# A seven-product feed-forward on one NeuronCore: six PSUM banks, norm matmuls placed later, and the last pass's operands made a pass ahead

## The chip, the core and the metric

The kernel runs on one core of a Trainium2 chip. The core's engines run side by side and meet through semaphores: TensorE (PE: matmuls, and PEld its weight loads), VectorE (DVE), ScalarE (ACT), GpSimd (POOL) and SyncE (SP), which here issues nearly all transfers between device memory and the on-chip buffers. Matmuls write into PSUM, eight banks of 128 x 512 fp32; all other operands lie in SBUF. The metric is the device time of one execution in microseconds. Three executions of the kernel before took 2996.5, 3001.04 and 3000.42 us; the median is 3000.42.

## What is computed

One layer of a decoder trunk on 2048 prompt tokens and 32 sample tokens, width 1024, all in fp32:

```python
sh1, sc1, g1, sh2, sc2, g2 = adaln_mods(c, lw['w_ada'], lw['b_ada'])
h = rms_norm(x, lw['norm1_g']) * (1 + sc1) + sh1
m, states = mixer(h)
x = x + g1 * m
h2 = rms_norm(x, lw['norm2_g']) * (1 + sc2) + sh2
x = x + g2 * swiglu(h2, lw['w_ffn_in'], lw['w_ffn_out'])
```

The mixer is one input projection, then sliding-window attention beside a gated causal convolution, a merge of the two and an output projection. swiglu(h) is (silu(g) * u) @ w_ffn_out, with g and u the halves of h @ w_ffn_in and 2816 hidden columns. A final RMSNorm closes it.

## The kernel before

**Numbers.** An fp32 matmul is made of three: each operand is split into a high half that the matmul takes exactly and the low rest, and hi x hi, hi x lo and lo x hi are summed in one PSUM bank (gemm, L483). The split of a weight is an ACT copy (L236, wh) and a POOL subtract (L237, wl).

**Stages.** Tokens come in two groups: g=0 has 1024 tokens, g=1 has 1024 and the 32 samples. For each group come the input projection, attention and convolution, and mixer_out (L1398), whose last product "wo" goes through three chunks of columns and leaves x2, the input of the feed-forward, in the tiles called third, or spilled to device memory as x2s. The feed-forward runs in three passes over the tokens: pass 0 holds chunks 0 and 1 of group 0 (2 x 336 columns), pass 1 chunk 2 of group 0 and chunk 0 of group 1, pass 2 chunks 1 and 2 of group 1 (2 x 352 columns each). Pass 0 runs ahead of group 1's mixer.

**Seven products.** A pass treats its two column blocks and the two halves of the 1024 input rows as a 2 x 2 block matrix, and the two halves of w_ffn_in likewise, and multiplies them with seven products in place of eight. For each hidden tile f, f_gate (L1735) makes products p1, p2, p6, p7, p5, p3, p4 in this order, each 4 x 3 = 12 matmuls into one bank, and VectorE adds them up into u, ga and ub on the way out of the bank. Weight combinations (the sums s and wr, w_part, L261) are made by VectorE from the raw weight when it has landed; the combinations of the activations, seven operands of four row tiles with a high and a low half each, are made once a pass by f_build (L1653) from the normed x2. f_down (L1781) takes pairs of hidden tiles through w_ffn_out: 16 banks of 6 matmuls, each added into x2 (residual, L1515). The blocks run as G1 (f_gate) of tiles 2p, then G2 (f_down) of pair p-1, then G1 of 2p+1 (ffn_order, L437).

**Norms.** The RMS of a chunk is a set of small matmuls of the squares sq with mean_d (rv_gen, L1564), a power on POOL, a diagonal matrix dg on VectorE, and a matmul with ones that spreads the factors over the partitions (f_rows, L1585). f_value (L1596) makes one normed, modulated tile of x2. h_second (L824) is the same for the input norm of group 1, in three chunks.

**PSUM.** Pool mm has four banks (all gemms, products and f_down tiles), ps two (norms, finals) and pt two (transposes: attention, x blocks, finals). A tile of a pool waits until the one that last had its bank has been read.

**What sets the order.** The order on each engine is written out by the program: the generators run in steps, one step wherever pump() (L452) is called, which is after every product or bank. Background generators (bg) step while a model of VectorE's time is not too far ahead of a model of PE's; tasks step once in task_dt ns of PE's modelled time. A "yield None" means that a generator waits for the next call. Instructions stand on an engine in the order in which they are issued, so a later yield puts an instruction behind more matmuls. All PE and VectorE operations go through one wrapper and have line 98 in the profile, so tiles' names tell them apart. After the last f_down of passes 0 and 1, the final norm of that pass's columns (final, L1858) runs as a task beside the next stage: transposes into a ps and a pt bank, squares on ACT, power on POOL, then scaling by ACT (L1894) and POOL (L1895, y) and stores on SP. At the last block but one of pass 1, build_next(2) (L1642) starts f_build(2), whose x2 fetches are issued by ACT (x2_fetch, L1615).

## Time and profile before

| | |
|---|---|
| median of three runs | 3000.42 us (2996.5 to 3001.04) |
| profiled execution, own time | 2991.93 us |
| its span, first to last instruction | 2989.8 us |
| mean granted PE clock | 0.971 of full |
| entry into pass 0 | about 700 to 780 us |
| steady pass 0 | 780 to 1200 us |
| first norm of group 1 begins | about 1200 us |
| entry into pass 1, steady | 1860 to 1950, 1950 to 2400 us |
| entry into pass 2, steady | 2400 to 2530, 2530 to 2900 us |

The page of the profile lists busy time of each engine, the span in 40 slices, the DMA queues, the chain of work that ended last and the costliest groups of instructions. Views of the trace add busy time in chosen stretches, what ended the waits of one engine in a stretch (engine, tile and line it waited for, us in total, times, longest), the chain in order of time, and the instructions in order of time. A wait is put down to the operation that came last. Shape: the slices of PE show the stage boundaries as dips between long stretches near full use:

```profile
PE   8988899999899999897889999799999977999998
PEclk9999999999999999998999999999999998999999
```

### The profile page before, as it was taken

The page shows a single profiled execution, that of the slowest core. Times are in us where ns is not written, and L with a number is a line of the kernel's source. Part 1 is how long each engine was busy: PE and PEld are TensorE (multiplying, and loading weights), DVE is VectorE, ACT ScalarE, POOL GpSimd, SP SyncE. Part 2 cuts the span into 40 slices and gives each one's busy share as a digit, 9 for nine tenths or more (in the row PEclk, how much of TensorE's full clock was granted, in tenths as well). Part 3 has the DMA queues.
Part 4 walks back from the last instruction along what each step waited for, and adds up shares of the span by engine and source line. Part 5 has one row for each costly group of instructions (what it writes and reads, how often), then busy time and mean ns, then how long its engine had stood idle before and what let it go on. Part 6 is the DMA issues. An engine that isn't in the chain of part 4 may idle for free. (4 is left out here: it accounts for less than half of the span.)

```text
span 2989.8 us, 43420 instructions
## 1 busy us (share of the span) xinstructions
PE 2743.9 (92%) x16046; PEld 2572.6 (86%) x16046; DVE 2054.2 (69%) x3320; ACT 1187.0 (40%) x2410; POOL 1649.5 (55%) x1289
## 2 busy tenths in 40 slices
PE   8988899999899999897889999799999977999998
PEld 4766677888799999897888999799999967999998
DVE  5999952466756666779997345766666676677676
ACT  4333465433433333432655343443333334333333
POOL 1366766333766567455674212476655647656654
PEclk9999999999999999998999999999999998999999
DMA  7542223443222222431112344332222224222222
GB/s 278 160 109 65 85 85 106 151 134 115 79 81 68 71 78 71 132 94 38 47 58 79 93 135 144 115 109 71 78 64 71 78 89 127 71 71 71 78 64 68
DMA packets 348472, 282.74 MB, mean 95 GB/s; under 512 B 31691, under 2 KB 304983, under 8 KB 348237
## 3 DMA queue, kind: packets, MB, share of 16 engines
q1 hardware_dynamic: 329189, 252.94, 27.6%
q10 hardware_dynamic: 19072, 27.03, 2.8%
q8 instruction: 127, 2.08, 0.3%
q14 instruction: 84, 0.69, 0.1%
HBM read 239.89 MB, written 40.14 MB: 94 GB/s over the span
## 5 line engine op out<-in xcount | busy, mean ns | idle before, releaser
L237 POOL TENSOR_TENSOR wl<-wr,wh 128x512 fp32r<-128x512 f32 (+1 forms) x470 | 890.1, 1908 | 684.6 <-ACT wh L236 624.5
L98 PE MATMUL mm<-third,wh 128*128 128x352 f32 (+1 forms) x3512 | 863.9, 326 | 60.8 <-DVE u L98 31.7
L98 PEld LDWEIGHTS mm<-third,wh 128*128 128x128 f32 x3512 | 615.9, 190 | 77.8 <-DVE u L98 40.0
L98 PE MATMUL mm<-third,wl 128*128 128x352 f32 (+1 forms) x1796 | 580.3, 323 | 0.0
L236 ACT ACTIVATE wh<-wr 128x512 fp32r<-128x512 f32 (+1 forms) x470 | 372.8, 811 | 373.0 <-PE mm L98 211.0
L98 PE MATMUL mm<-hh,wh 128*128 128x352 f32 (+1 forms) x1200 | 435.5, 363 | 28.8 <-DVE u L98 9.1
L98 PE MATMUL mm<-mh,wh 128*128 128x352 f32 (+1 forms) x1396 | 450.7, 323 | 4.3 <-DVE third L98 1.7
L98 PE MATMUL mm<-ml,wh 128*128 128x352 f32 (+1 forms) x1396 | 444.9, 322 | 0.0
L98 PE MATMUL mm<-hh,wl 128*128 128x352 f32 (+1 forms) x1200 | 425.5, 355 | 0.0
L237 POOL TENSOR_TENSOR wl<-s,wh 128x512 fp32r<-128x512 f32 x198 | 255.8, 1301 | 292.5 <-ACT wh L236 292.5
L98 PE MATMUL mm<-hl,wh 128*128 128x352 f32 (+1 forms) x1200 | 415.6, 355 | 0.6 <-DVE hl L98 0.6
L98 DVE SCALAR_TENSOR_TENSOR third<-mm,mod_G,third 128x352 f32<-128x352 f32 (+2 forms) x576 | 315.2, 568 | 143.8 <-PE mm L98 121.8
L98 DVE SCALAR_TENSOR_TENSOR dw<-u,cw,dw 128x1024 f32<-128x1024 f32 x240 | 395.2, 1660 | 4.7
L98 PE MATMUL mm<-mh,wl 128*128 128x336 f32 (+1 forms) x1044 | 334.9, 321 | 7.6 <-POOL wl L237 7.6
L98 PEld LDWEIGHTS mm<-third,wl 128*128 128x128 f32 x1796 | 341.2, 190 | 0.0
L98 DVE TENSOR_TENSOR u<-mm,u 128x352 f32<-128x352 f32 (+1 forms) x330 | 168.2, 515 | 165.8 <-PE mm L98 158.5
L98 PEld LDWEIGHTS mm<-hh,wh 128*128 128x128 f32 x1200 | 229.7, 191 | 60.7 <-issue 11.3
L236 ACT ACTIVATE wh<-s 128x512 fp32r<-128x512 f32 x198 | 120.7, 626 | 394.9 <-PE mm L98 251.5
L98 PEld LDWEIGHTS mm<-mh,wh 128*128 128x128 f32 x1396 | 265.5, 190 | 6.5 <-DVE third L98 2.0
L98 PEld LDWEIGHTS mm<-ml,wh 128*128 128x128 f32 x1396 | 264.1, 190 | 0.0
L98 PEld LDWEIGHTS mm<-hh,wl 128*128 128x128 f32 x1200 | 228.9, 191 | 21.6
L98 PEld LDWEIGHTS mm<-hl,wh 128*128 128x128 f32 x1200 | 228.2, 192 | 22.4 <-DVE hl L98 1.2
(333 smaller groups left out, 4288.2 us busy)
## 6 DMA issues: line engine op xcount, KB each, us to landing
wr<-in_w_ffn_in SPq DMA_DIRECT2D x132, 512.0 KB
wr<-in_w_ffn_out SPq DMA_DIRECT2D x66, 512.0 KB
wr<-in_w_in SPq DMA_DIRECT2D x52, 512.0 KB
wr<-in_w_ada SPq DMA_DIRECT2D x48, 512.0 KB
wr<-in_w_out SPq DMA_DIRECT2D x32, 512.0 KB
gl<-gate SPq DMA_DIRECT2D x64, 176.0 KB
gate<-gst ACTq DMA_DIRECT2D x48, 176.0 KB
xt<-in_x_prompt SPq DMA_DIRECT2D x16, 512.0 KB
```

The costliest lines, as they stand in the source:

```text
L98: return f(*args, **kw)
L236: self.nc.scalar.activation(out=hi, in_=src, func=AF.Copy)
L237: self.nc.gpsimd.tensor_tensor(out=lo, in0=src, in1=hi.bitcast(F32), op=ALU.subtract)
```

## The change

- f_gate's products and f_down's tiles take their banks from bank(), which gives mm, mm, pt in turn, so that they turn over six banks.
- In the last chunk of wo a step is made in the middle of each product and one after it.
- h_second makes its three diagonals first and waits two steps before each spreading matmul. rv_gen waits two steps (six for chunk 2) ahead of the mean_d matmuls and two before it reports; f_rows waits two steps between diagonal and matmul.
- f_ahead is a task that starts at G1 of tile 1 of pass 1, one step every 5500 ns. From the spilled x2 it makes pass 2's seven operands, one row tile after the other, through single buffers hi and lo, and stores them in 56 DRAM tiles of 176 KB. It keeps both ps banks for the two spread factors (ra, rb), and uses the buffers kg, mask, kh and kl of the attention.
- f_reload stands in the place of f_build(2): 56 loads on SP, no arithmetic. Before it starts, the remaining tasks are run to their end.

```diff
+        self.op_d = {name: [[self.dram(f"op_{name}{k}{i}", (128, 352)) for i in range(2)] for k in range(4)] for name in PRODUCTS}
...
+    def bank(self):
+
+        self.banks += 1
+        return self.mm() if self.banks % 3 else self.pt()
...
+            if mid and i == 3 * n // 2 - 1:
+                self.pump()
...
-            yield None
+            rbs.append(dg)
+        for i, (c0, cw) in enumerate(GROUPS[1]["chunks"]):
+            for _ in range(2):
+                yield None
+            dg = rbs[i]
             ps = self.ps()
             self.T.matmul(ps[:, :cw], self.ones, dg[:, :cw], start=True, stop=True)
             self.V.tensor_copy(dg[:, :cw], ps[:, :cw])
-            rbs.append(dg)
+        dg = ps = None
...
-            self.gemm_group([("wo", g, m)], mv, g, partial(wo_evac, part=(2,)), chunks=chunks[2:])
+            u, ev = self.w_next(("wo", g, m)), wo_evac(("wo", g, m), (2,))
+            ps = self.gemm_tile(u, mv, *chunks[2], mid=True)
+            ev(ps, *chunks[2])
+            self.w_done()
+            self.pump()
...
-        yield None
+        for _ in range(6 if ci == 2 else 2):
+            yield None
...
+        for _ in range(2):
+            yield None
         self.rv_done.add((g, ci))
...
-    def f_rows(self, p, e):
-
-        P = PASSES[p]
-        cw, src = P["cw"], P["src"][e]
+    def f_rows(self, src):
+
+        cw = GROUPS[src[0]]["out"][src[1]][1]
         while src not in self.rv_done:
             yield None
         toks = self.tok_tiles(0, 0, cw)
         dg = self.diag(self.rv[:, src[0] * 3 + src[1]], 0, toks)
-        yield None
+        for _ in range(2):
+            yield None
         self.f_rb = self.diag_bcast(dg, toks)
...
+    def f_ahead(self):
+
+        nc, V = self.nc, self.V
+        sa, sb = PASSES[2]["src"]
+        yield from self.f_rows(sa)
+        ra = self.f_rb
+        yield 0
+        yield from self.f_rows(sb)
+        rb = self.f_rb
+        self.f_rb = None
+        s0, s1, s2 = (self.kg[:, i * 352:i * 352 + 352] for i in range(3))
+        s3 = self.mask[:, :352]
+        hi, lo = (t.rearrange("p a b -> p (a b)")[:, :352] for t in (self.kh, self.kl))
+
+        def load(t, src, f):
+            nc.sync.dma_start(out=t, in_=self.x2_d[src][f])
+
+        def out(name, k, v):
+            nc.scalar.activation(out=hi, in_=v, func=AF.Copy)
+            nc.gpsimd.tensor_tensor(out=lo, in0=v, in1=hi.bitcast(F32), op=ALU.subtract)
+            yield 0
+            for t, d in zip((hi, lo), self.op_d[name][k]):
+                nc.sync.dma_start(out=d, in_=t.bitcast(F32))
+            yield 0
+
+        def minus(o, x, y):
+            V.tensor_tensor(out=o, in0=x, in1=y, op=ALU.subtract)
+        for k in range(4):
+            load(s0, sa, k)
+            load(s1, sb, k)
+            load(s2, sb, k + 4)
+            load(s3, sa, k + 4)
+            yield 0
+            self.f_value(s0, s0, sa, k, ra)
+            yield from out("p1", k, s0)
+            self.f_value(s1, s1, sb, k, rb)
+            minus(s0, s1, s0)
+            yield from out("p5", k, s0)
+            self.f_value(s2, s2, sb, k + 4, rb)
+            minus(s1, s2, s1)
+            yield from out("p7", k, s1)
+            yield from out("p3", k, s2)
+            minus(s0, s2, s0)
+            yield from out("p6", k, s0)
+            self.f_value(s3, s3, sa, k + 4, ra)
+            yield from out("p2", k, s3)
+            minus(s3, s3, s0)
+            yield from out("p4", k, s3)
+
+    def f_reload(self):
+
+        for name in PRODUCTS:
+            self.h2[name] = []
+            for k in range(4):
+                while True:
+                    hl = self.r_take(352)
+                    if hl:
+                        break
+                    yield None
+                for t, d in zip(hl, self.op_d[name][k]):
+                    self.nc.sync.dma_start(out=t.bitcast(F32), in_=d)
+                self.h2[name].append(tuple(hl))
+                hl = t = None
+                if k % 2:
+                    yield 0
+            self.h2_n += 1
+        self.raw_extra = True
+        self.rl = []
...
-        if p == 2:
-            self.x2_order = [((1, 1), f) for f in range(KD)] + [((1, 2), f) for k in range(4) for f in (k, k + 4)]
         self.xs = []
         self.x2_fetch(0)
-        self.bg.append(self.f_build(p))
+        self.bg.append(self.f_reload() if p == 2 else self.f_build(p))
...
-            ps = self.mm()
+            ps = self.bank()
...
-                ps = self.mm()
+                ps = self.bank()
...
+                if p == 1 and key[1] == 1:
+                    self.task_dt = 5500
+                    self.tasks.append(self.f_ahead())
...
                 elif p == 1:
+                    while self.tasks:
+                        self.step(self.tasks)
                     self.room -= 1
                     a_new = self.a_new
                     self.build_next(2)
```

In the code, L98 is the wrapper, wr a raw weight, third the x2 tiles or operands, op_p the new DRAM tiles. Three places of the order follow, each with the line of its own kernel.

VectorE where mixer_out of group 0 ends and pass 0 begins; rv and dg are the norm's factors and diagonals, sq the squares, and third<-third,mod_A is the making of operands. Before:

```order
L98 TENSOR_SCALAR rv<-ps 128x2
L98 TENSOR_SCALAR rv<-ps 80x1
L98 TENSOR_TENSOR dg<-ident,rv 128x256
L98 TENSOR_SCALAR dg<-ident,rv 80x80
L98 SCALAR_TENSOR_TENSOR third<-mm,mod_G_156,third 128x336
L98 TENSOR_TENSOR sq<-sq,sqt 128x336
L98 SCALAR_TENSOR_TENSOR third<-third,mod_A_158,ps 128x336 x8
```

After the change:

```order
L98 TENSOR_TENSOR sq<-sq,sqt 128x336
L98 TENSOR_SCALAR rv<-ps 128x2
L98 TENSOR_SCALAR rv<-ps 80x1
L98 SCALAR_TENSOR_TENSOR third<-mm,mod_G_156,third 128x352
L98 TENSOR_TENSOR dg<-ident,rv 128x256
L98 TENSOR_SCALAR dg<-ident,rv 80x80
L98 TENSOR_SCALAR rv<-ps 128x2
L98 TENSOR_SCALAR rv<-ps 80x1
L98 SCALAR_TENSOR_TENSOR third<-mm,mod_G_156,third 128x352
L98 TENSOR_TENSOR sq<-sq,sqt 128x352
L98 SCALAR_TENSOR_TENSOR third<-third,mod_A_158,ps 128x336 x8
```

The first norm's factors have moved behind the last 336-column tiles, the diagonal no longer follows them at once, and the first operands stand behind tiles of the third chunk.

TensorE at the first tile of pass 2, with the transposes of the second final (ident) and the product p6 behind them. Before:

```order
L98 MATMUL ps<-ident,third 128x128 x4
L98 MATMUL pt<-ident,third 128x128 x4
L98 MATMUL mm<-third,wh 128x352 x2
L98 MATMUL mm<-third,wl 128x352
L98 MATMUL mm<-third,wh 128x352 x2
```

After the change:

```order
L98 MATMUL ps<-ident,third 128x128 x4
L98 MATMUL pt<-ident,third 128x128 x4
L98 MATMUL pt<-third,wh 128x352 x2
L98 MATMUL pt<-third,wl 128x352
L98 MATMUL pt<-third,wh 128x352 x2
```

The rows stand at the same place; p6 has moved from an mm bank to one of the two pt banks that the finals use too.

SyncE from the end of pass 1 into pass 2, where wr are weights, gf the final norm's gains and out_y_prompt the finals' stores. Before:

```order
L341 DMA wr<-in_w_ffn_in 128x8x128 x4
L1844 DMA gf<-in_final_norm_g 128x1024
L1900 DMA out_y_prompt<-y 128x512 x2
L341 DMA wr<-in_w_ffn_in 128x8x128
L1900 DMA out_y_prompt<-y 128x512 x2
```

After the change:

```order
L347 DMA wr<-in_w_ffn_in 128x8x128 x3
L1690 DMA third<-op_p 128x352 x50
L347 DMA wr<-in_w_ffn_in 128x8x128
L1932 DMA gf<-in_final_norm_g 128x1024
L1988 DMA out_y_prompt<-y 128x512 x2
L1690 DMA third<-op_p 128x352 x6
L347 DMA wr<-in_w_ffn_in 128x8x128 x2
L1988 DMA out_y_prompt<-y 128x512 x2
```

Fifty reloads now stand ahead of the fourth weight, and the last six behind the first final's two stores.

More of the change, by code (lines that the diff above doesn't have):

```diff
@@ L155, in __init__ @@
         self.pairs, self.half, self.raw_live, self.raw_extra = 0, None, {"wr": 0, "slot": 0}, False
-        self.room = 0
+        self.room = self.banks = 0
+        self.op_d = {name: [[self.dram(f"op_{name}{k}{i}", (128, 352)) for i in range(2)] for k in range(4)] for name in PRODUCTS}
     def dram(self, name, shape):
@@ L480, in run, with gemm @@
             pass
-    def gemm(self, ps, cw, terms, hi_first=False):
+    def gemm(self, ps, cw, terms, hi_first=False, mid=False):
         n = len(terms)
@@ L491, in gemm, with gemm_tile @@
             self.T.matmul(ps[:, :cw], w, x, start=(i == 0), stop=(i == 3 * n - 1))
-    def gemm_tile(self, unit, act, c0, cw, nk=8, mo=0, hi_first=False):
+            if mid and i == 3 * n // 2 - 1:
+                self.pump()
+    def gemm_tile(self, unit, act, c0, cw, nk=8, mo=0, hi_first=False, mid=False):
         wh = unit[0].rearrange("p (k m) -> p k m", k=nk)
@@ L498, in gemm_tile @@
         self.gemm(ps, cw, [(wh[:, k, s], wl[:, k, s], act[k][0][:, c0:c0 + cw], act[k][1][:, c0:c0 + cw]) for k in range(nk)],
-                  hi_first)
+                  hi_first, mid)
         return ps
@@ L1510, in mixer_out @@
         for m in range(8):
-            self.gemm_group([("wo", g, m)], mv, g, partial(wo_evac, part=(2,)), chunks=chunks[2:])
+            u, ev = self.w_next(("wo", g, m)), wo_evac(("wo", g, m), (2,))
[3 more added lines that the diff above has]
+            self.pump()
+        u = ev = ps = None
         chunk_done(2)
@@ L1592, in f_rows, with f_value @@
         dg = self.diag(self.rv[:, src[0] * 3 + src[1]], 0, toks)
-        yield None
+        for _ in range(2):
+            yield None
         self.f_rb = self.diag_bcast(dg, toks)
-    def f_value(self, t, p, e, f, rb):
-        P = PASSES[p]
-        cw, src = P["cw"], P["src"][e]
+    def f_value(self, t, x, src, f, rb):
+        cw = t.shape[1]
         smp = src == (1, 2)
         pw = cw - NS if smp else cw
-        if p == 2 or src == (0, 2):
-            x = self.x2_fetch()
-        else:
-            x = self.x2_of[src][f]
         A, B = self.mods["A2"], self.mods["B2"]
@@ L1668, in minus @@
             V.tensor_tensor(out=out, in0=x, in1=y, op=ALU.subtract)
-        yield from self.f_rows(p, 0)
+        sa, sb = PASSES[p]["src"]
+        yield from self.f_rows(sa)
         rb = self.f_rb
@@ L1673, in f_build @@
             a.append((yield from piece()))
-            self.f_value(a[f][0], p, 0, f, rb)
+            self.f_value(a[f][0], self.x2_fetch() if p == 1 else self.x2_of[sa][f], sa, f, rb)
             yield 0
@@ L1678, in f_build @@
         yield from self.f_split("p2", a[4:], Q)
-        yield from self.f_rows(p, 1)
+        yield from self.f_rows(sb)
         rb = self.f_rb
@@ L1683, in f_build @@
             b2.append((yield from piece()))
-            self.f_value(b1, p, 1, k, rb)
-            self.f_value(b2[k][0], p, 1, k + 4, rb)
+            self.f_value(b1, self.x2_of[sb][k], sb, k, rb)
+            self.f_value(b2[k][0], self.x2_of[sb][k + 4], sb, k + 4, rb)
             yield 0
```

## The prediction

> **What bounds the kernel now.** I read the page first. Its columns are busy time, share of the span and instructions of each engine.
>
> ```profile
> span 2989.8 us, 43420 instructions
> PE 2743.9 (92%) x16046; PEld 2572.6 (86%) x16046; DVE 2054.2 (69%) x3320; ACT 1187.0 (40%) x2410; POOL 1649.5 (55%) x1289
> ```
>
> TensorE is the bound: 92%, 246 us idle in the span, and no other engine above 69%. So the change is worth what it takes out of PE's idle time. To see where that idle time lies I took busy time by stretches. Columns: stretch and length, busy time (instructions) of PE, weight load, DVE, ACT, POOL, then PE's granted clock, DMA share, GB/s.
>
> ```profile
> 700.00:780.00 80.00, 62.87 (x361) 60.21 (x360) 65.32 (x95) 39.91 (x79) 47.31 (x35) 0.89 0.34 104
> 780.00:1200.00 420.00, 401.93 (x2567) 396.48 (x2565) 264.76 (x407) 146.53 (x263) 278.50 (x204) 0.99 0.25 75
> 1200.00:1230.00 30.00, 22.52 (x120) 20.71 (x119) 22.95 (x48) 9.08 (x14) 11.57 (x6) 0.89 0.41 125
> 1860.00:1950.00 90.00, 70.03 (x418) 68.00 (x417) 62.54 (x104) 39.11 (x76) 43.51 (x29) 0.93 0.39 123
> 1950.00:2400.00 450.00, 439.86 (x2689) 434.68 (x2689) 284.17 (x430) 156.77 (x278) 286.01 (x213) 0.99 0.27 80
> 2400.00:2530.00 130.00, 90.00 (x512) 85.49 (x510) 91.80 (x162) 55.93 (x121) 76.56 (x62) 0.88 0.37 113
> 2550.00:2600.00 50.00, 48.80 (x302) 48.24 (x301) 36.15 (x65) 16.41 (x29) 29.52 (x23) 1.00 0.25 74
> ```
>
> The 700, 1860 and 2400 rows are the entries into passes 0, 1 and 2; the 1200 row is the start of the second group's first norm; the others are steady. In steady work a matmul takes 48.80 / 302 = 0.1616 us. The 512 matmuls of 2400 to 2530 would take 82.7 us at that pace, so this entry loses 47.3 us, and the clock of 0.88 beside the idle time is part of it. Next, what ended PE's waits (total us, times, longest), one fence for each steady part and each entry:
>
> ```profile
> PE mm L98 <- DVE third L98: 8.5, 9, 1.0
> PE mm L98 <- DVE u L98: 7.9, 9, 1.4
> ...
> PE mm L98 <- DVE u L98: 10.1, 9, 1.2
> ...
> PE mm L98 <- DVE u L98: 9.4, 8, 1.2
> ```
> ```profile
> PE ps L98 <- DVE dg L98: 11.8, 3, 8.6
> PE mm L98 <- ACT third L1636: 11.1, 1, 11.1
> PE mm L98 <- DVE u L98: 6.9, 3, 4.4
> PE ps L98 <- ACT y L1894: 6.9, 2, 5.0
> PE mm L98 <- DVE third L98: 4.3, 3, 2.6
> ```
>
> The first fence is 800 to 1200 (pass 0, two rows), 1960 to 2390 (pass 1), 2540 to 2900 (pass 2): about one stall of 1 us in every pair of ffn tiles, 8.5 + 7.9 + 10.1 + 9.4 = 35.9 us in all. The second is 2390 to 2550. Then the waits of the other two entries, 700 to 860 and 1700 to 1960, and of 1200 to 1300:
>
> ```profile
> PE ps L98 <- DVE dg L98: 6.8, 2, 5.7
> PE ps L98 <- DVE sq L98: 6.7, 1, 6.7
> ...
> PE ps L98 <- DVE dg L98: 8.2, 1, 8.2
> PE ps L98 <- DVE sq L98: 5.3, 1, 5.3
> ...
> PE ps L98 <- DVE dg L98: 4.3, 2, 3.9
> ```
>
> **1. Six banks, steady parts.** The chain of waits shows one pair of pass 2 (start, us, engine and line):
>
> ```profile
> 2611.40 3.85 DMA wr<-in_w_ffn_in
> 2615.27 1.77 DVE s L98
> ...
> 2617.12 1.61 DVE wr L98
> 2618.76 0.70 DVE s L98
> 2619.48 0.69 DVE s L98
> 2620.17 0.44 DVE u L98
> 2620.66 34.91 PE mm L98 x214
> ...
> 2664.86 34.95 PE mm L98 x214
> ```
>
> A raw weight lands, VectorE makes the Strassen sums of it (s, wr, s, s), and behind these in its queue stands u, which empties a product's bank; PE wants that bank. A pair is 7 x 12 x 2 matmuls of products and 96 of f_down, 264 in all, 42.7 us at 0.1616; its period on the chain is 44.2 us (2664.86 after 2620.66), so PE stands 1.2 to 1.5 us. With six banks PE writes two products, 2 x 12 x 0.1616 = 3.9 us, before it needs that bank. The stall of 1.2 us is smaller. But is there a second loop behind it? DMA, the four sums and u take 9.1 us, and the buffer's refill starts from the same sums; between the point where they may start and the next use lie 62 matmuls of the pair, 10.0 us. The loop fits, with under 1 us to spare. I take 33 of the 35.9 us: **-33** (pass 0 about 14, pass 1 10, pass 2 9). Bounds: 0 if the loop holds after all, -36 if nothing is left.
>
> **2. Entry into pass 2.** f_build(2) goes, with its diagonal broadcasts, its splits and the 16 fetches of x2; 56 loads of finished operands stand in its place. Of the waits at 2390 to 2550, dg (11.8), the split (11.1) and third (4.3) go, 27.2 us. The wait of ps on y stays: the final norm's transposes lie at the same places. The 6.9 on u stay too, part weight and part bank. Of the other 6.3 us of the 47.3, the slow clock, I take 5 with the waits that caused it: **-32**, 15 left. What could be late next is the reload:
>
> ```profile
> 2403.33 0.37 SPq L341 DMA_DIRECT2D wr<-in_w_ffn_in  x1
> 2510.59 10.81 SPq L1856 DMA_DIRECT2D third<-x2s  x16
> 2496.16 4.32 DMA out_y_prompt<-y
> ```
>
> SP issues a 176 KB load in 10.81 / 16 = 0.676 us, so 56 take 38 us. The reload stands behind the weight issued at 2403.33; PE still has two f_down blocks of pass 1 then, 192 matmuls or 31 us, and the last product needs its operands 84 x 0.1616 = 13.6 us after that: about 2404 to 2446 against 2404 to 2448. It fits, barely; the last six loads stand behind the first output store, which waits for the final norm, and this I carry as part of the 15 us left. Bounds -42 (5 left) and -5 (rival C).
>
> **3. The new finals' bank.** p6 of pass 2's first tile now lies in pt, in the bank that the first final must leave:
>
> ```profile
> 2455.29 0.60 PE L98 MATMUL pt<-ident,third 128*128 128x128 f32 x4
> 2459.49 0.68 ACT L1894 ACTIVATE y<-pt,fs 128x512 f32<-128x512 f32 x1
> ```
>
> From the transposes to the last read of pt is 2460.17 - 2455.29 = 4.9 us; between the first final and p6 PE has p2, 1.9 us, and the second final's eight transposes, about 1.2 us. So some 2 us a final could be lost where before the two banks each of ps and pt turned among finals alone, at 6.9 us in all. I leave the 6.9 in place and take nothing more; the upper bound is rival C.
>
> **4. f_ahead in pass 1.** It adds 28 ACT copies, 28 POOL subtracts, 16 values and 12 subtracts of s on DVE, 16 loads and 56 stores, spread by its pace of 5.5 us a step over more than 60 steps. Nearest rows (us total, mean ns, idle before):
>
> ```profile
> L98 DVE TENSOR_TENSOR u<-mm,u 128x352 f32<-128x352 f32 x220 | 112.9, 520 | 107.9 <-PE mm L98 102.2 <-POOL wl L237 2.0
> L98 DVE TENSOR_TENSOR u<-u,ga 128x352 f32<-128x352 f32 x44 | 52.2, 1186 | 4.4
> L98 DVE SCALAR_TENSOR_TENSOR third<-xx,mod_A,ps 128x352 f32<-128x352 f32 x16 | 8.5, 577 | 5.6 <-DMA xx<-x2s 3.4 <-PE mm L98 2.2
> L1637 POOL TENSOR_TENSOR third<-third 128x352 fp32r<-128x352 f32 x10 | 10.5, 1079 | 12.7 <-ACT third L1636 12.7
> ```
>
> POOL gets 28 x 1.08 = 30 us, DVE 16 x 0.58 + 12 x 1.19 = 24 us, in some 370 us. The 1950 to 2400 row has DVE at 63% and POOL at 64%: both have room. The cost can only be a DVE operation in front of a u, at most 1.19 us each, against a bank cushion that term 1 has just widened by 1.9 us a bank. I take **+5**, bounds 0 and 28 x 0.58 = 16. The two broadcasts' waits move here as well, in the midst of matmuls, with two steps between diagonal and matmul. Beside the rows: the Trainium skill, "SBUF — State Buffer", section "Who interferes with whom", says VectorE's second read port is shared with GpSimd under an exclusive lock, so that a two-SBUF-input VectorE operation and a GpSimd one block each other. The trace agrees as far as 520 ns with a PSUM input and 1186 ns with two from SBUF; by that rule each of the 28 added POOL subtracts could hold a VectorE operation for its 1.08 us, 30 us of VectorE's time, much of which would reach PE. By that rule the sum would be up to 25 us worse, by the room in the rows 0.
>
> **5. Norm matmuls behind their operands.** At the entry to pass 0 the dg and sq waits are 13.5 of 17.1 us idle. The first norm's matmul now comes 50 matmuls (8 us) later, but DVE is busy 65.32 of 80, so what PE no longer waits for there it partly waits for at the operands: **-5**, bounds 0 and -14. Entry to pass 1: dg and sq 13.5 of 20.0 us, DVE busy only 62.54 of 90, so **-7**, bounds 0 and -16. The second group's norm (4.3 us on dg, three broadcasts moved 4 to 9 matmuls): **-3**, bounds 0 and -4. The halved gap between steps in the last chunk of wo costs nothing; PE's matmuls are the same and only the background's steps move.
>
> **Sum.** -33 - 32 + 5 - 5 - 7 - 3 = -75 us, on the profiled execution (2991.93 us, span 2989.8): 2917. The median of the runs shown, 3000.42, lies 8.5 above that execution; with it the forecast is **2925**.
>
> **Rivals.**
> - *B: banks don't help.* The bank wait goes and PE stands at the weight instead; the period of 44.2 us stays since DVE's sums and POOL's lower halves set it. For it: the spare of under 1 us. Against it: DVE 36.15 and POOL 29.52 of 50 us busy in the 2550 row, so no engine is full. Without term 1's 33: 2958.
> - *C: the wait at pass 2's entry only moves,* to finals that hold pt and a reload in the queue with weights and outputs behind it. All six finals late by a store's landing of about 4.5 us: 2925 + 27 = 2952.
> - *D: slower.* f_ahead has one hi and one lo buffer; ACT's next copy waits until both stores of the one before have landed, and behind that copy on ACT stand the weights' wh copies, which PE needs. An out is two steps, so one comes every 2 x 5.5 = 11 us, and the banks give 3.9 us more (term 1's two products). With POOL's 1.1 us in each, a landing up to 13.8 us is covered; from 13.8 + 80 / 28 = 16.7 us on it eats the 80 us of the other terms and decides. At 17 us: 28 x (17 + 1.1 - 14.9) = 90, 3000 - 80 + 90 = 3010. Against it: the store row above lands in 4.32 us, and the DMA share is 0.27.
> - *G: the contention in pass 1 is real.* Each of the 28 added POOL subtracts holds a VectorE operation with two SBUF inputs for its 1.08 us, in front of a u, and all of it reaches PE: +30 in place of +5, 2950. For it: 1186 against 520 ns in the rows of term 4. Against it: only part of DVE's operations have two SBUF inputs.
> - *E: all goes,* each term at its lower bound: 3 more in term 1, 10 in term 2, 5 in term 4, 9 + 9 + 1 in term 5: 2888.
> - *F: nothing happens.* The steps' delays move waits to other instructions of the same chains and the total stays: 3000. Against it: 11.8 + 11.1 us at one place whose work is gone from there.
>
> **How the numbers follow.** The forecast 0.56 (its own terms' spread 2900 to 2950), B 0.10, C 0.11, G 0.07, E 0.08, D 0.05, F 0.03. A measurement of this kernel can tell about 0.2%, 6 us, from no change. Faster by more: forecast, B, C, G, E, 0.92; same: F, 0.03; slower: D, 0.05. The range reaches past B, C and G above and to E below: 2886 to 2970; outside lie D, F and the outer tails.
>
> **What would show it.** In 800 to 1200, 1960 to 2390 and 2540 to 2900 the waits on u and third fall below 3 us in sum and a pair's period is 42.7 to 43; if it is 44 with waits on wl or wr, B holds. At pass 2's entry the waits on dg and on ACT's split are gone; if new waits on DMA third<-op or on ACT y exceed 15 us, C holds. In pass 1 a wait of ACT on the stores of op, followed by PE on wh, is D. The forecast fails most likely where several parts meet: the pt bank shared by finals and products, and the SP queue at the entry into pass 2.

## The result, and the profile after

The changed kernel takes 2931.36 us (median of four, 2930.97 to 2936.75) beside 3000.73 for the kernel before: a ratio of 0.9774 (in brackets, here and below, the 95% interval: 0.9757 to 0.9791), 69 us or 2.3% faster. The forecast was 2925. The sum came out almost right, but its terms did not: one was more than half again too small, two were too large on the side of the gain, and these errors nearly cancelled. Between the two profiled executions, on which the sum was worked out, the gain is 61 us (2991.93 to 2930.97). The page of the changed kernel, its first lines:

```profile
span 2927.8 us, 43739 instructions
PE 2738.3 (94%) x16046; PEld 2573.8 (88%) x16046; DVE 2039.0 (70%) x3304; ACT 1187.1 (41%) x2410; POOL 1672.8 (57%) x1305
```

The matmuls are the same 16046 in number, and PE's idle time in the span fell from 246 to 189.5 us. Busy time fell by 5.6 us for the same matmuls; below, matmuls are seen to take longer just behind a stall and at a lower granted clock. The waits of PE in what was the steady part of pass 1 and in the entry into pass 2 (1940 to 2340 and 2330 to 2500 here, since everything lies 15 to 20 us earlier):

```profile
PE mm L98 <- DVE u L98: 8.2, 8, 2.5
PE mm L98 <- DVE third L98: 2.7, 1, 2.7
...
PE pt L98 <- ACT y L1982: 5.3, 2, 4.9
PE mm L98 <- DVE u L98: 4.7, 2, 4.3
PE pt L98 <- DVE u L98: 3.9, 1, 3.9
```

The waits on dg and on ACT's split are gone from the entry, as forecast. In the steady part of pass 2 (2490 to 2850) PE waits for nothing at all. In pass 0 (800 to 1200) 4.8 us on u and third are left, 3.0 of them one wait in its first tiles, at 811. But in pass 1, where six banks were to take 10 us of stalls away, 10.9 us are left, 3.1 of them in its first tiles, at 1958 and 1977.

To read where time went I matched the two traces by the count of matmuls: at the moment at which the kernel before had started n matmuls, how much earlier had the other started as many? The difference between two marks is what a stage saved. This holds to about 2 us a stage. The table has it for the changed kernel and for the runs below (marks in the time of the kernel before):

| us saved in | 650-850, entry pass 0 | 850-1190, pass 0 | 1190-1860, mixer | 1860-1960, entry pass 1 | 1960-2390, pass 1 | 2390-2540, entry pass 2 | 2540-2890, pass 2 |
|---|---|---|---|---|---|---|---|
| the change | 1.0 | 17.8 | -2.7 | 6.2 | -2.2 | 31.3 | 13.0 |
| banks alone (e1) | 0.2 | 17.8 | -0.8 | 1.0 | 15.0 | 6.1 | 12.9 |
| no banks (e2) | -2.7 | -5.5 | -1.2 | 2.7 | -23.2 | 31.0 | 0.9 |
| no f_ahead (e3) | -3.2 | 18.1 | -2.3 | 6.3 | 10.3 | 6.1 | 12.9 |
| norm steps alone (e4) | -1.5 | -8.9 | -1.2 | 1.3 | 0.4 | 2.8 | 0.2 |
| lower halves on VectorE (e5) | -1.8 | 17.0 | -1.0 | 5.3 | -7.7 | 32.2 | 13.6 |
| finer steps (e6) | 2.1 | 17.0 | -1.6 | 5.8 | -1.4 | 30.9 | 13.9 |
| no norm steps (e7) | -0.5 | 17.8 | 0.7 | 1.5 | 7.1 | 30.8 | 13.0 |
| no lower halves in f_ahead (e8) | 0.1 | 17.0 | 0.3 | 5.5 | 3.7 | 31.6 | 13.7 |
| no VectorE work in f_ahead (e11) | -0.6 | 18.3 | -0.5 | 6.3 | 9.3 | 30.8 | 13.0 |
| steps held back (e9) | -0.1 | 18.9 | -2.2 | 7.3 | 3.5 | 29.5 | 13.3 |
| held back, no norm steps (e10) | 0.5 | 16.9 | -0.4 | 0.2 | 5.1 | 31.5 | 13.4 |
| held back, mm at the entry (e12) | -0.9 | 18.1 | 0.0 | 5.6 | 3.8 | 34.2 | 13.2 |

### The profile page after: what moved, and what is told of

Read it like the earlier page. It is cut to its first block, busy times and chain, and to the rows that moved or that the text cites. A ratio compares the mean times of both kernels' runs of the same rounds, so it can differ in the third digit from the quotient of the medians.

```text
span 2927.8 us, 43739 instructions
## 1 busy us (share of the span) xinstructions
PE 2738.3 (94%) x16046; PEld 2573.8 (88%) x16046; DVE 2039.0 (70%) x3304; ACT 1187.1 (41%) x2410; POOL 1672.8 (57%) x1305
## 3 DMA queue, kind: packets, MB, share of 16 engines
q1 hardware_dynamic: 347621, 276.02, 30.8%
## 5 line engine op out<-in xcount | busy, mean ns | idle before, releaser
L98 PE MATMUL mm<-third,wh 128*128 128x352 f32 (+1 forms) x2323 | 568.4, 325 | 6.6 <-DVE u L98 3.7
L98 PE MATMUL mm<-hh,wh 128*128 128x352 f32 (+1 forms) x1200 | 436.0, 363 | 30.5 <-DVE u L98 11.2
L98 PE MATMUL mm<-hh,wl 128*128 128x352 f32 (+1 forms) x1200 | 426.4, 355 | 0.0
L98 PEld LDWEIGHTS mm<-third,wh 128*128 128x128 f32 x2323 | 407.7, 190 | 12.1 <-DVE third L98 6.6
L98 PE MATMUL mm<-hl,wh 128*128 128x352 f32 (+1 forms) x1200 | 416.6, 356 | 1.3 <-DVE hl L98 1.3
L98 DVE SCALAR_TENSOR_TENSOR dw<-u,cw,dw 128x1024 f32<-128x1024 f32 x240 | 393.4, 1652 | 4.7
L98 PE MATMUL mm<-third,wl 128*128 128x352 f32 (+1 forms) x1187 | 383.2, 323 | 0.6 <-POOL wl L243 0.6
L98 PE MATMUL mm<-mh,wh 128*128 128x352 f32 (+1 forms) x1048 | 340.1, 325 | 3.4 <-DVE third L98 1.8
L98 PE MATMUL mm<-ml,wh 128*128 128x352 f32 (+1 forms) x1048 | 334.8, 324 | 4.2 <-ACT wh L242 2.5
L98 PE MATMUL pt<-third,wh 128*128 128x352 f32 (+1 forms) x1189 | 292.2, 325 | 10.9 <-ACT y L1982 5.3
L98 DVE SCALAR_TENSOR_TENSOR third<-mm,mod_G,third 128x352 f32<-128x352 f32 (+2 forms) x408 | 223.7, 565 | 95.5 <-PE mm L98 78.3
L98 PEld LDWEIGHTS mm<-hh,wh 128*128 128x128 f32 x1200 | 230.1, 192 | 63.2 <-DVE u L98 12.1
L98 PE MATMUL mm<-mh,wl 128*128 128x336 f32 (+1 forms) x824 | 266.1, 323 | 5.7 <-POOL wl L243 5.7
L98 PEld LDWEIGHTS mm<-hl,wh 128*128 128x128 f32 x1200 | 228.8, 192 | 22.9 <-DVE hl L98 1.9
L98 PEld LDWEIGHTS mm<-hh,wl 128*128 128x128 f32 x1200 | 229.3, 191 | 21.5
L98 PEld LDWEIGHTS mm<-third,wl 128*128 128x128 f32 x1187 | 225.3, 190 | 0.9 <-POOL wl L243 0.9
L98 PEld LDWEIGHTS pt<-third,wh 128*128 128x128 f32 x1189 | 209.8, 191 | 12.7 <-ACT y L1982 5.8
L98 PEld LDWEIGHTS mm<-mh,wh 128*128 128x128 f32 x1048 | 200.3, 191 | 4.6 <-DVE third L98 2.1
```

The costliest lines, as they stand in the source:

```text
L98: return f(*args, **kw)
```

## The experiments

### The three parts of the change, apart

e1 is the kernel before with bank() alone:

```diff
-            ps = self.mm()
+            ps = self.bank()
             self.f_product(ps, name, p, f)
...
-                ps = self.mm()
+                ps = self.bank()
```

> The kernel before with the six-bank rotation alone. Theory of the prediction: the steady stalls go in all three passes (14 + 10 + 9 us), 3000.7 - 33 = about 2968, and in the profile no wait on u over 0.3 us in the steady parts of passes 0, 1 and 2. Rival B (the loop of DMA and DVE holds the period): within 6 us of 3000, pair period 44.2 us in pass 2. Rival of the price in pass 1 being the banks' own fault (the profile of the changed kernel still has 10.9 us of stalls in pass 1): pass 1 keeps its 10 us here too, though nothing is added there, and the time is about 2978.

e2 is the changed kernel with the four banks back:

```diff
-        return self.mm() if self.banks % 3 else self.pt()
+        return self.mm()
```

> The changed kernel with products and f_down tiles in the four mm banks as before. If the terms add up as in the prediction: 2931 + 33 = 2964. If f_ahead's work costs pass 1 all that the banks gave there, and as much again without their cushion: the pass 1 stalls rise from 10.9 to about 20 us, and the time is again about 2931 + 12 + 10 + 14 = 2967. If the six banks are worth nothing in pass 1 in any case (rival): stalls there stay at 11 us and the time is about 2931 + 12 + 14 = 2957.

e3 is the changed kernel with f_build(2) and its fetches back:

```diff
-        self.bg.append(self.f_reload() if p == 2 else self.f_build(p))
+        self.bg.append(self.f_build(p))
...
-                if p == 1 and key[1] == 1:
-                    self.task_dt = 5500
-                    self.tasks.append(self.f_ahead())
```

> The changed kernel with f_build(2) back at the entry into pass 2 and no f_ahead (six banks and norm steps kept). Theory of the prediction: the pair is worth -32 at the entry and +5 in pass 1, so 2931 + 27 = 2958. Theory from the profile of after: f_ahead costs pass 1 about 10 us, so 2931 + 31 - 10 = 2952, and the stalls of the steady part of pass 1 fall from 10.9 us to under 3. Rival (pass 1's stalls have nothing to do with f_ahead): they stay at 9 us or more and the time is 2960 or more.

e4 is e3 with the four banks of e2, so that only the norm steps and the step inside wo's products are left of the change.

> The norm steps and the step in the middle of wo's last products alone (four banks, f_build(2), no f_ahead). Theory of the prediction: -5 at the entry to pass 0, -7 to pass 1, -3 at the second group's norm: about 2986. Rival (the waits move to other links of the same chain): within 6 us of 3000. The profile of after suggests little at the entry to pass 0 and 5 us at the entry to pass 1.

| run | median us | ratio to before |
|---|---|---|
| before, beside these | 2999.89 | |
| e1, banks alone | 2946.22 | 0.9821 (0.9799 to 0.9844) |
| e2, all but the banks | 2984.22 | 0.9951 (0.9937 to 0.9964) |
| e3, all but f_ahead | 2943.20 | 0.9809 (0.9784 to 0.9834) |
| e4, norm steps alone | 2998.38 | 1.0002 (0.9987 to 1.0016) |

**The banks are worth 54 us alone, not 33.** Every theory of e1 was too small. e2 came out above its three theories (2957 to 2967) and e3 below its three (2952 to 2960). **The norm steps are worth nothing measurable alone,** not 15. **f_ahead with f_reload is worth 12 with six banks** (2943.2 to 2931.4) **and 14 with four** (2998.4 to 2984.2), not 27. The table says where: at the entry it saves 25 with six banks (31.3 against 6.1) and 28 with four (31.0 against 2.8), but it costs pass 1 12.5 us with six banks (10.3 against -2.2) and 23.6 with four (0.4 against -23.2). Busy time by stretch shows it plainest; in 1980 to 2330 before, changed, banks alone, and without banks (columns as in the prediction):

```profile
1980.00:2330.00 350.00, 341.05 (x2095) 336.59 (x2094) 216.75 (x335) 116.77 (x206) 212.91 (x159) 1.00 0.24 73
```
```profile
1980.00:2330.00 350.00, 342.57 (x2096) 339.39 (x2096) 244.66 (x385) 134.75 (x248) 244.15 (x185) 0.99 0.35 106
```
```profile
1980.00:2330.00 350.00, 350.00 (x2176) 350.00 (x2175) 222.66 (x345) 120.78 (x214) 220.23 (x165) 1.00 0.24 73
```
```profile
1980.00:2330.00 350.00, 329.62 (x1989) 325.91 (x1987) 239.01 (x372) 130.24 (x238) 237.58 (x179) 0.98 0.33 103
```

With six banks alone PE does not stand for a moment: 2176 matmuls in place of 2095, 81 x 0.1608 = 13 us. f_ahead takes all of that back (2096), and without the cushion it goes to 1989, where the lower clock of 0.98 has a share too (0.02 x 350, an estimate of 7 us). So the banks and f_ahead do not add up stage by stage: in pass 1 the banks pay for f_ahead.

**Why the banks gave more than the waits listed.** The listed waits of the steady parts were 35.9 us, and the stages saved 17.8 + 15.0 + 12.9 = 45.7. The main reason is that a listed wait is less than what a stall costs. In the kernel before, the order of time around one stall of pass 2 (start, us, instruction; in brackets the idle time before it):

```profile
2619.15 0.32 PE L98 MATMUL mm<-third,wl 128*128 128x352 f32 x1
2620.66 0.43 PE L98 MATMUL mm<-third,wh 128*128 128x352 f32 x1 [1.19 <-DVE u L98]
2620.93 0.32 PE L98 MATMUL mm<-act,wh 128*128 128x352 f32 x1
```

From start to start it is 1.51 and then 0.27 us, where 0.16 each is the pace: 1.46 us lost for a listed 1.19, and about 2 us later two more starts come 0.29 and 0.26 us after the one before. Over 1960 to 2390, the distances above 0.25 us between starts exceed the pace by 14.8 us in all in the kernel before, for 10.1 us of listed waits; in the same matmuls of e1 it is 0.1. That is the 15.0 us of pass 1, at a granted clock of 1.00 (so it is in 2540 to 2900). In the kernel before, the clock comes on top in pass 0 only. There the stalls come in twos. Such a pair in e4, and busy time in e4 behind that pair and over the whole of pass 0:

```profile
897.68 0.58 PE L98 MATMUL mm<-third,wh 128*128 128x336 f32 x2 [1.11 <-DVE u L98]
899.82 0.93 PE L98 MATMUL mm<-third,wh 128*128 128x336 f32 x2 [0.95 <-DVE third L98]
```
```profile
900.00:903.50 3.50, 3.50 (x14) 3.50 (x15) 1.77 (x5) 0.00 (x0) 1.23 (x2) 0.54 0.07 20
900.00:910.00 10.00, 10.00 (x56) 10.00 (x57) 5.81 (x12) 1.15 (x2) 3.77 (x4) 0.84 0.02 7
910.00:920.00 10.00, 10.00 (x67) 10.00 (x66) 5.64 (x8) 3.13 (x6) 5.49 (x4) 1.00 0.15 54
...
850.00:1150.00 300.00, 287.30 (x1780) 283.43 (x1779) 183.64 (x287) 97.17 (x174) 181.96 (x136) 0.96 0.22 70
```

PE is busy throughout 900 to 910, yet does 56 matmuls in place of 67, with the clock at 0.84: after the second gap it runs at about half the clock for 3.5 us. The same row of the kernel before, and of the changed kernel:

```profile
850.00:1150.00 300.00, 287.61 (x1831) 284.04 (x1832) 184.53 (x292) 101.38 (x181) 190.04 (x140) 0.99 0.25 73
```
```profile
850.00:1150.00 300.00, 298.18 (x1932) 296.00 (x1931) 196.77 (x314) 104.73 (x187) 196.25 (x146) 1.00 0.26 76
```

The kernel before and e4 idle as much (12.4 and 12.7 us), but e4 starts 51 matmuls fewer, at a mean clock of 0.96 against 0.99: at 0.16 us each that is most of the 8.9 us by which e4 lies behind in pass 0. This is no effect of the norm steps, which move nothing in that stage. The kernel before itself took 2988.5 to 3005.3 us in the 19 executions beside e1 to e4, at mean clocks of 0.971 down to 0.965, and its profiled execution, the zero of the table, is one of the better ones (0.971). So the four-bank rows of the table, e2 and e4, hold some us of chance where there are stalls. With the stalls gone the clock stays at 1.00.

### What f_ahead costs in pass 1

e5 makes the lower halves on VectorE, e8 leaves them out, e6 cuts the steps finer (value, bias, difference, hi, lo and stores each in a step of their own, 2500 ns), and e7 takes the norm steps out:

```diff
-            nc.gpsimd.tensor_tensor(out=lo, in0=v, in1=hi.bitcast(F32), op=ALU.subtract)
+            V.tensor_tensor(out=lo, in0=v, in1=hi.bitcast(F32), op=ALU.subtract)
```

> The changed kernel with f_ahead's 28 lower halves subtracted on VectorE in place of GpSimd. It costs 2931 with 7.4 us of PE idle in pass 1's steady part (342.6 of 350 us busy, where the runs without f_ahead have 350.0). Theory W (waits at the head of a queue: an f_ahead instruction stands on its engine waiting for the one before it in its chain, and the weights' work behind it is late): the wait on ACT's kh moves to VectorE, where the products' u stand behind it, so more stalls on u and 5 to 15 us slower, 2936 to 2946. Theory G (GpSimd's added subtracts hold VectorE's two-input operations): without them pass 1 gains most of its 12, 2920 to 2925. Theory O (plain occupancy of GpSimd in front of the weights' wl): GpSimd's 30 us go, about 2925.

```diff
-            nc.gpsimd.tensor_tensor(out=lo, in0=v, in1=hi.bitcast(F32), op=ALU.subtract)
             yield 0
             for t, d in zip((hi, lo), self.op_d[name][k]):
```

> The changed kernel without the 28 lower-half subtracts of f_ahead (this part of the computation is left out: the stored lower halves are what the buffer held). Theories G and O: GpSimd's 30 us go from pass 1 and with them most of the price, 2920 to 2924. Theory W: only the wait of GpSimd on kh goes; ACT's own waits on kg, kh and the stores, with the weights' copies behind them, stay, and so does half or more of the price: 2925 to 2930.

```diff
+                V.tensor_tensor(out=v, in0=x, in1=y, op=ALU.subtract)
+                yield 0
             nc.scalar.activation(out=hi, in_=v, func=AF.Copy)
+            yield 0
             nc.gpsimd.tensor_tensor(out=lo, in0=v, in1=hi.bitcast(F32), op=ALU.subtract)
             yield 0
...
-                    self.task_dt = 5500
+                    self.task_dt = 2500
```

> The changed kernel with f_ahead's steps cut finer, the same arithmetic: value, bias, difference, hi, lo and the stores are each issued a step (2500 ns) after the one they wait for, four values ahead of the seven outs. Theory W: the waits of GpSimd on kh (42.7 us) and of ACT on kg and kh (35 us and 14 us on the stores) fall below 15 us in sum, pass 1 gets back 6 to 12 of its 12 us, about 2922. Theories G and O (the work itself, not the waits): pass 1's PE idle stays at 6 us or more and the time within 5 us of 2931.

```diff
-        for _ in range(6 if ci == 2 else 2):
-            yield None
+        yield None
...
-            ps = self.gemm_tile(u, mv, *chunks[2], mid=True)
+            self.gemm_group([("wo", g, m)], mv, g, partial(wo_evac, part=(2,)), chunks=chunks[2:])
```

> The changed kernel without the norm steps and without the step inside wo's last products (six banks and f_ahead with f_reload kept). Theory of the prediction: those are worth 15 us, so 2946. Theory from the four-bank run of the norm steps alone, which came out level (1.0002): 2931 within 4. Theory from the stages of the six-bank runs with and without them: 5 us at the entry to pass 1, so about 2936.

Measured (median us; ratio and its interval): e5 2935.97 (0.9784, 0.9758 to 0.9810), e6 2929.81 (0.9767, 0.9744 to 0.9789), e7 2927.22 (0.9756, 0.9733 to 0.9778), e8 2923.54 (0.9743, 0.9722 to 0.9763). e5 is 5 us slower, with PE busy 337.90 us in 1980 to 2330 in place of 342.57. That is at the low end of theory W, the waits at the head of a queue, and against G and O, by which it should have been faster. e6 does not bear W out in full. The waits that it named, in 1980 to 2330 of the changed kernel and of e6:

```profile
ACT kh L1648 <- DVE kg L98: 18.3, 8, 7.4
ACT kg L1628 <- DVE kg L98: 17.0, 6, 6.8
...
POOL kl L1649 <- ACT kh L1648: 41.2, 23, 5.9
```
```profile
ACT kh L1652 <- DVE kg L98: 9.7, 3, 5.0
...
POOL kl L1654 <- ACT kh L1652: 4.0, 4, 1.3
```

GpSimd's wait went from 41 to 4 us and ACT's on kg from 35 to 10 (on the stores 14 us became 18), and pass 1 still saves -1.4 us in place of -2.2. So most of these waits cost nothing: they are idle time on an engine that nobody waits for just then. But W keeps a share, which is seen when the column of pass 1 is cut at 2000 us (from the start of each matmul; the sums lie within 0.4 us of the table above):

| us saved in | 1960-2000 | 2000-2390 |
|---|---|---|
| the change | -3.0 | 0.4 |
| banks alone (e1) | 1.6 | 13.3 |
| no f_ahead (e3) | -2.8 | 13.2 |
| lower halves on VectorE (e5) | -3.0 | -4.6 |
| finer steps (e6) | -4.8 | 3.4 |
| no norm steps (e7) | -0.4 | 7.5 |
| no lower halves in f_ahead (e8) | -1.7 | 5.4 |
| steps held back (e9) | -3.8 | 7.5 |
| no VectorE work in f_ahead (e11) | -3.0 | 12.2 |

All that f_ahead costs, 12.8 us, lies behind 2000, and e6 gives back 3.0 of it. What e6 loses ahead of 2000 is a new wait: at its quicker pace PE comes to f_ahead's own norm factors before their diagonals are made.

```profile
1947.80 1.60 PE L98 MATMUL ps<-dg,ones 128*128 128x256 f32 x4 [3.85 <-DVE dg L98]
```

Taking GpSimd's work away (e8) gives pass 1 back 6 of 12.5 us; so theories G or O had a part, and no run tells the two apart. Without the norm steps (e7) the same f_ahead costs pass 1 only 15.0 - 7.1 = 7.9: it depends on how its steps fall. e7 also settles the norm steps beside six banks: 2927.2 against 2931.4, intervals that overlap; there is no gain from them, and they may cost a few us.

To find the rest, e11 leaves out f_ahead's VectorE work, with GpSimd's, ACT's and all transfers kept:

```diff
-            self.f_value(s1, s1, sb, k, rb)
+            nc.scalar.activation(out=s1, in_=s1, func=AF.Identity, bias=self.mods["B2"][:, k, 0:1])
...
-            V.tensor_tensor(out=o, in0=x, in1=y, op=ALU.subtract)
+            pass
```

> The changed kernel without f_ahead's VectorE work: the normed values and the differences of the operands are left out, x2 plus the shift is split and stored in place of all seven operands. Without GpSimd's part the time was 2923.5, half of the 12 us. If VectorE's added work in front of s and u is the other half: 2923 to 2926, and the two halves add up. If VectorE's added work costs nothing (it stands in its idle gaps): 2931 within 3.

2918.70 (0.9734, 0.9712 to 0.9757), less than either theory, and its stretch:

```profile
1980.00:2330.00 350.00, 350.00 (x2166) 349.06 (x2165) 224.28 (x347) 138.08 (x254) 246.03 (x191) 1.00 0.36 109
```

GpSimd has 246 us of work and the transfers 109 GB/s, as in the changed kernel, and PE is busy all the time. **So without VectorE's part there are no stalls in this stretch**; GpSimd's share shows only where VectorE's is there too. e11 takes two things away, VectorE's 20 us of work (244.66 against 224.28) and most of the waits of ACT and GpSimd for its results. By e6, which shortened those waits, some 3 us are theirs; the rest is not parted further.

How it comes about is seen in the order of time before one stall of the changed kernel (at 2197.78 PE had waited 1.61 us for u):

```profile
2180.22 0.53 DVE L98 TENSOR_TENSOR kg<-kg 128x352 f32<-128x352 f32 x1
2181.35 1.19 POOL L1649 TENSOR_TENSOR kl<-kg,kh 128x352 fp32r<-128x352 f32 x1 [1.32 <-ACT kh L1648]
2184.11 4.58 SPq L347 DMA_DIRECT2D wr<-in_w_ffn_in  x2
2185.86 6.04 POOL L243 TENSOR_TENSOR wl<-wr,wh 128x1024 fp32r<-128x1024 f32 x3
2189.39 0.54 DVE L98 SCALAR_TENSOR_TENSOR kg<-kg,mod_A,ps 128x320 f32<-128x320 f32 x1
...
2192.04 0.53 DVE L98 TENSOR_TENSOR kg<-kg 128x352 f32<-128x352 f32 x1
2192.77 0.69 DVE L98 TENSOR_TENSOR s<-wr 128x512 f32<-128x512 f32 x1 [0.20 <-DMA wr<-in_w_ffn_in]
...
2195.64 1.65 DVE L98 TENSOR_TENSOR s<-wr,s 128x512 f32<-128x512 f32 x1
2197.22 0.51 DVE L98 TENSOR_TENSOR u<-mm,u 128x352 f32<-128x352 f32 x1
```

u stands on VectorE behind the sums of a raw weight, from 2192.77 on. One step of f_ahead, five operations (kg; the 32 sample columns have three of their own), stands in front of them, but it was over at 2192.57, and the sums then waited 0.20 us for the weight. So here the weight is late. It is the second of the two loads from 2184.11, issued at 2188.3, when the first of GpSimd's three wl from 2185.86 on was done with its buffer. GpSimd had worked without a gap since 2181.35, and there it had begun with f_ahead's lower half, 1.19 us, for which it had stood 1.32 us: that waited for ACT's high half, and this for VectorE's step before, at 2180.22. At this stall, then, f_ahead's price came in by the queue of GpSimd, as theory W has it. This chain is read from the order of time of one stall, not tested apart. By it the loop goes from wl by the weight's transfer and s to u, with the under 1 us of spare that the prediction estimated, and f_ahead's work can enter it in front of wl or in front of s.

e9 and e10 test this by where the steps stand: none in the first G1 of a pair, which f_down follows, and one each 3500 ns in the rest. e10 is e9 without the norm steps.

```diff
-        if self.tasks and self.T.t >= self.task_t:
+        if self.tasks and not self.hold and self.T.t >= self.task_t:
...
+                self.hold = p == 1 and key[1] > 1 and key[1] % 2 == 0
                 self.f_gate(p, key[1])
+                self.hold = False
```

> The changed kernel with f_ahead's steps held back in the first G1 of each pair of pass 1 (whose end is followed by f_down) and issued every 3500 ns in the rest. Nearly all stalls of pass 1 lie at the first f_down matmuls, behind u, s and the landing of a raw weight. Theory L (f_ahead costs only where its work stands in the loop from wl by the weight's DMA and s to u before f_down): pass 1 gets back 6 to 11 of its 12 us, 2920 to 2925, PE 347 of 350 us busy or more. Theory C (any added work costs, wherever it stands: contention of VectorE and GpSimd, and transfers): the stalls move to the other half of the pair and the time stays within 4 of 2931.

> The same hold, without the norm steps and the step inside wo's last products. Without the norm steps the changed kernel took 2927. Theory L: 4 to 8 us less than that, about 2921. Theory C: 2927 within 4.

e9 took 2923.57 (0.9748, 0.9720 to 0.9776), e10 2925.19 (0.9759, 0.9735 to 0.9783). Pass 1 gets back 5.7 us (3.5 against -2.2), as theory L has it, but PE is busy 345.32 of 350 us, not the 347 of theory L. By theory C the stalls would have moved to the other half of the pair. They have not: counted in matmuls, those that are left (at 2068 and 2152, 1.4 and 1.8 us) stand in f_down as before, at its ninth and its sixth bank, where the changed kernel has them at the sixth and eighth. Neither theory holds alone. e10 has no gain over e7, 2925.2 against 2927.2 with intervals that overlap, as theory C has it.

### The rest of the entry into pass 2

e12 is e9 with the products of pass 2 kept to the mm banks while finals are still to come:

```diff
-            ps = self.bank()
+            ps = self.mm() if p == 2 and self.tasks else self.bank()
             self.f_product(ps, name, p, f)
```

> The kernel with the hold (2923.6), and in pass 2 the products keep to the four mm banks as long as finals are still waiting to be issued, so that no product waits for a pt bank that a final holds. At that entry the changed kernel shows a product in pt waiting 4.9 us on a final's scaling (y) and a final's transposes in pt waiting 3.9 us on a product's u. If these two waits are what the shared pt banks cost (a part of rival C): 4 to 8 us less, 2916 to 2920. If the wait only goes to another link (mm banks behind the same VectorE queue, SyncE's queue of reloads): 2924 within 3.

2920.44 (0.9740, 0.9725 to 0.9754): 3 us less than e9, with intervals that overlap, and between its two theories. The entry saves 34.2 in place of 29.5 us. But the waits of PE in 2330 to 2500, e9 and then e12, have for the most part only changed places:

```profile
PE mm L98 <- DVE u L98: 5.5, 1, 5.5
PE pt L98 <- ACT y L1985: 5.3, 2, 4.9
PE pt L98 <- DVE u L98: 3.7, 1, 3.7
```
```profile
PE ps L98 <- ACT y L1985: 6.8, 2, 5.8
PE mm L98 <- DVE u L98: 6.3, 1, 6.3
```

The waits at pt are gone, 9.0 us, but PE waits 6.8 us on y at ps in their place, and 14.5 us in all became 13.1. The granted clock in 2360 to 2500 was 0.95 in place of 0.93, an estimated 3 us of the 140; whether that comes from the change or by chance is not shown. e12 is the fastest kernel that computes everything; its interval lies just below that of the change. What is left at the entry is a queue. SyncE in the changed kernel:

```profile
2393.72 19.48 SPq L1690 DMA_DIRECT2D third<-op_p  x38
...
2466.07 0.40 SPq L347 DMA_DIRECT2D wr<-in_w_ffn_in  x1
2466.56 7.75 SPq L1944 DMA_DIRECT2D third<-x2s  x16
2474.41 9.02 SPq L347 DMA_DIRECT2D wr<-in_w_ffn_in  x3
```
```profile
2480.07 0.69 DVE L98 TENSOR_TENSOR s<-wr 128x512 f32<-128x512 f32 x1 [7.61 <-DMA wr<-in_w_ffn_in]
```

The reload is no trouble: 38 loads go out in 19.48 us, 0.51 us each. But the raw weight issued at 2474.41 waits in the queue behind the 16 loads of x2, VectorE waits 7.61 us for it, and u behind it gives PE the stall of 4.3 us. This was so before too; that it could be cured by placing those loads elsewhere was not tried.

## Why the prediction came out right, and where its steps failed

- **The sum** was -75 and the result -69. The banks brought 21 more than forecast, f_ahead with f_reload 15 less and the norm steps 15 less. That these nearly cancel is luck, and so is another 8 us: the sum was worked out on the profiled execution, 2991.93 to 2917, and the 8.5 us by which the median lay above it were added to the changed kernel too. That kernel's profiled execution took 2930.97, 14 more than 2917, and its median lies only 0.4 above it. A right total is no proof of its terms.
- **Term 1, six banks, -33: right mechanism, mis-sized.** Alone -54; in the steady stages -45.7, and -6 at the entry into pass 2, where u had been left in place. The 15 of pass 1 are paid out again, 12.5 to f_ahead and 4.7 to the norm steps. The step that failed is adding up listed waits, "I take 33 of the 35.9 us". The same paragraph had the better figure: a period of 44.2 against 42.7 us is 1.5 us a pair. And -36 was no bound, since a wait lists less than a stall costs.
- **Rival B** is out: with e1 nothing is left of the waits in pass 1, so the loop of transfer and sums did fit into its 10.0 us. That f_ahead hit at its small spare is what the one stall read above suggests.
- **Term 2, the entry, -32: right.** 31.3, and 31.0 with four banks (e2); the 6 us that the banks bring here alone do not come on top. "It fits, barely" was too careful; the loads were issued in 0.51 and not 0.676 us.
- **Term 3 and rival C: half right.** A product waits 4.9 us at pt for a final's y, once and not six times. Taken away from there (e12), most of the wait turned up at ps.
- **Term 4, f_ahead, +5: the step that failed.** It cost 12.5. "Both have room" was read from shares of busy time; "the cost can only be a DVE operation in front of a u" left out GpSimd's queue, whose work gone gives 6 us back (e8); and the cushion of the banks was counted as still there after term 1 had left, by its own estimate, under 1 us of spare in the loop behind it. The 7.9 of e7 and 12.5 of the changed kernel lie inside its bounds of 0 and 16, the 23.6 without banks does not.
- **Rival G,** and the rule of the Trainium skill, "SBUF — State Buffer", section "Who interferes with whom", beside it: no run here shows that the lock costs this kernel time. With all 28 added GpSimd subtracts and no added VectorE work (e11) there is no stall in 1980 to 2330, so rival G as it was put, with the subtracts alone, is out. The 6 us of e8 could be the lock between the subtracts and VectorE's added work, or plain occupancy of GpSimd; that is open. Single operations are longer: ub<-ub,u took 512 ns with banks alone, and with GpSimd's added work 857 ns (e11); but others became shorter by about as much (rows of 1980 to 2330, banks alone and e11):

```profile
L98 DVE TENSOR_TENSOR u<-u,ga 128x352 f32<-128x352 f32 x16 | 19.0, 1190 | 1.7
L98 DVE TENSOR_TENSOR ub<-ub,u 128x352 f32<-128x352 f32 x16 | 8.2, 512 | 0.0
```
```profile
L98 DVE TENSOR_TENSOR u<-u,ga 128x352 f32<-128x352 f32 x16 | 14.7, 917 | 1.7
L98 DVE TENSOR_TENSOR ub<-ub,u 128x352 f32<-128x352 f32 x16 | 13.7, 857 | 0.0
```

- **Rival D** is out: ACT waited 14 us on the stores in 1980 to 2330, and e11, which keeps them and waits 17 us, has no stall there.
- **Term 5, the norm steps, -15: wrong.** The waits moved on, as rival F said for the whole. At the entry to pass 0 those on dg and sq fell from 13.5 to 4.1 us (690 to 860), but PE now waits 3.6 us for ACT's mh, among others, and the stage saves 1.0 where 5 were forecast. At the entry to pass 1 the steps do save 5 us (6.3 against 1.0), and in the first tiles behind it they lose them (1.6 against -2.8 up to 2000): e3, with six banks and no f_ahead, has just these two waits in 1955 to 2370, and e1 has none there.

```profile
1958.38 0.43 PE L98 MATMUL mm<-ml,wh 128*128 128x352 f32 x1 [0.80 <-DVE u L98]
1977.22 0.59 PE L98 MATMUL mm<-third,wh 128*128 128x352 f32 x2 [3.12 <-DVE u L98]
```

What exactly VectorE does in place of the norms there stays open; it was not taken apart.

## What to carry to other kernels

Size a stall by the period of its loop against the work in it, not by the listed waits: start-up of PE and a lower granted clock behind the stall come on top. Where one part of a change makes room in a loop and another adds work to that loop, count the room once; and ask of added work not what share of its engine is free, but what stands behind it in the queue at the tightest place. A wait in front of a matmul that is pushed later was here handed on to a later operand from the same engine: take work out, or move it to another stage, as f_reload does.

## What was not expected of the hardware

Gaps of PE of about 1 us, two of them with a dozen matmuls between, can be followed by 3.5 us at half the granted clock, 0.54 behind 1.11 and 0.95 us in e4. The length of the gaps does not decide it. In the kernel before, gaps of 0.81 and 0.93 us end at 852.56, and gaps of 0.82 and 0.95 us at 984.36; the 3.5 us behind each:

```profile
852.50:856.00 3.50, 3.44 (x12) 3.44 (x13) 1.99 (x5) 0.04 (x1) 1.46 (x2) 0.51 0.17 52
984.30:987.80 3.50, 3.44 (x22) 3.45 (x23) 2.83 (x6) 0.04 (x1) 1.47 (x2) 1.00 0.18 54
```

Two kernels with much the same waits in pass 0 differed by 9 us there through this alone (0.99 and 0.96 mean clock). What does decide it is not shown here.
